# A two-layer retention and linear-attention backbone on one core: broadcast conditioning loads, three shift chunks on TensorE, another order of the first loads

## The chip, the cores and the metric

The kernel runs on one core of a Trainium2 chip, in one launch. The metric is the device time of the whole program in microseconds (us), the median of several runs. Five engines work beside each other, each on its own queue in order: TensorE (PE in the views; its weight loads are PEld), VectorE (DVE), ScalarE (ACT), GpSimd (POOL) and SyncE (SP). Here SP issues all data DMAs. PE writes into PSUM, and ACT and DVE empty it.

## What is computed

There are 256 context tokens and 512 latent tokens of width 1024, and two layers. Each layer starts with a modulated RMSNorm whose shift and scale (and later a gate) come from a conditioning vector, one for the context and one for the latents:

```python
def modulation(cvec, w_ada, b_ada):
    m = jax.nn.silu(cvec) @ w_ada + b_ada
    return jnp.split(m, 3, axis=-1)
...
        shift_x, scale_x, gate_x = modulation(c, w_ada[l], b_ada[l])
        shift_c, scale_c, gate_c = modulation(c_ctx, w_ada[l], b_ada[l])
        u_ctx = rms_norm(h_ctx, norm_gain[l]) * (1.0 + scale_c) + shift_c
        ctx_parts, ctx_states = token_mixers(u_ctx, w_in[l], ret_decay[l], gla_w_up[l], gla_b_up[l],
                                             None, zero_states)
```

One projection of the result feeds a retention branch and a gated linear attention branch, both bidirectional; they are normalised, gated, projected, merged, projected once more and added to the residual. A last RMSNorm gives the output. All of it is float32.

## The kernel before

**Layout.** Activations lie transposed: features on the 128 partitions, in 8 chunks of 128 (four pairs kp), tokens along the free dimension in three groups g of 256 (0 is the context) or six tiles of 128. A product in full precision is made of three products of split operands: `split` (L359) makes a high part on ACT (a copy, tiles `whi`, `streamh`) and the rest on DVE (`wlo`, `streaml`), and `mm3` (L315) issues high by high, low by high, high by low. Where no split pays, PE multiplies float32 operands directly (`mm`, L309).

**Order of the work.** Nothing runs as written. Generators hand operations to a planner, `Emit` (L221); it keeps a clock for each engine from its own cost estimates, takes the generators by priority and writes the operations out in the order in which they become ready by those clocks. On the chip each engine then runs its list in that order and waits only on semaphores. SP's list is in order too, and a load waits there for the eighth load before it (one semaphore lane each).

**The start, which the change touches.** `main` (L1597) issues `small` (biases and gains, and c as columns) and `cst` (the identity among others), then the twelve loads of x, 256 KB each (L1618 on), chunk pair by chunk pair and all three groups of each. `Norm.add` (L643) squares each piece on ACT and adds it up on DVE; `Norm.finish` (L662) sums over partitions on PE, takes the power on POOL and broadcasts it on PE. The modulation of layer 0 comes in four steps kp. For each, `ada_load` (L750) fetches eight pieces: two chunks of the transposed w_ada (`adat`, for the shift) and two chunks of w_ada (`adas`, for the scale). `ada_first` (L758) makes the scale on PE, as eight float32 products with the two silu(c) columns as weights (`op`), a copy of the two rows to SBUF on ACT and a turn of each chunk by the identity; the shift is made on DVE, as eight products with a sum (`ada_dve`, L742), for which silu(c) must stand in every partition. That is `load_c` (L724): 16 float32 products of 128 columns broadcast silu(c) over the partitions, ACT empties them, and four DMAs write them to DRAM, from which `ada_late` (L797) loads them again, three times in the program, for the other modulation chunks (all on DVE). `make_u` (L690) then scales x, applies mulc and mods on ACT and splits into `streamh`/`streaml`.

**The first projection.** `rproj_outer` (L1092) is the first user: for each chunk k of 8, and each of the six token tiles, one `mm3` of 512 columns, 144 matmuls in all, with three `pj` and three `xp` buffers of PSUM open at once. `ret_evac` (L1047) empties them. `Weights` (L502) loads weights by pieces of 512 KB into two buffers `wraw` and splits them into nine `whi`/`wlo` pairs. `decays` (L1001) and the tables R.tab (`ret_setup`, L1020) need ACT functions of other tables, so ACT_TABLE_LOADs. From there on the program is a long row of such projections, with the scans in between.

The places that say what a sentence can't:

```python
                for k in range(4):
                    e.mm(o[0][:, k], sc[:, 4 * half + k, v:v + 1].to_broadcast([P, P]), ident, True, True)
                t = cr[2 * v + half]
                e.copy(t[0], o[0].rearrange("p k n -> p (k n)"))
...
            yield dict(ev=ada_ev[1])
            decays()
            yield dict(ev=ada_ev[3])
```

Of the kernel before, what the change touches and what calls it, by code (L numbers as in the profile page):

```python
# [19 lines left out]
P = 128  # L20
D = 1024
KC = D // P
# [78 lines left out]


SMALL = {}
_o = 0
for _n, _w in (("bada", DEPTH * 24), ("ngain", DEPTH * KC), ("rgain", DEPTH * KC), ("ggain", DEPTH * KC), ("fgain", KC),
               ("decay", DEPTH * 2 * H), ("cT", KC * 2), ("kpos", DEPTH * 2 * H), ("zm", 3), ("wm", 2)):
    SMALL[_n] = (_o, _w)
    _o += _w
NSMALL = _o


def host_arrays(x, c, ctx, c_ctx, norm_gain, w_ada, b_ada, w_in, ret_decay, gla_w_up, gla_b_up, ret_norm_gain,
# [6 lines left out]
    a["adat"] = np.ascontiguousarray(w_ada.transpose(0, 2, 1)).reshape(DEPTH, 24, P, D)  # L119
    a["adas"] = np.ascontiguousarray(  # L120
        w_ada[0][:, D:2 * D].reshape(KC // 2, 2, P, 4, 256).transpose(3, 0, 2, 1, 4).reshape(4 * KC // 2, P, 512))
    small = np.zeros((P, NSMALL), f)

    def put(name, v):
        o, w = SMALL[name]
        small[:, o:o + w] = v
# [375 lines left out]
class Weights:  # L502


    def __init__(self, e, plan, src, begun):
        self.e, self.plan, self.src, self.begun = e, plan, src, begun
        e.spawn(self.run(), WEIGHTS)

    def run(self):
# [62 lines left out]
def body(ctx, tc, io, out):  # L572
# [148 lines left out]

    crd = []
# [35 lines left out]
    def ada_first(kp, C, A, ev, begun):  # L758

        yield dict(ev=[A.ev])  # L760

        def pe():
            yield dict(op=2, g=1, ev=begun)
            m = e.get("op", (256,))
            for k in range(KC):
                r = A.sraw[k // 2]
                e.mm(m[0][0:2], sc[:, k], r[0][:, k % 2], k == 0, k == KC - 1)
                if k % 2:
                    e.free(r)
            row = e.get("g", (256,))  # L770
            e.copy(row[0][0:2], m[0][0:2])
            e.free(m)
            o = e.get("op", (2, 2))
            for i in range(2):
                e.mm(o[0][:, i], row[0][0:2, i * P:i * P + P], ident[0:2, 0:2], True, True)
            e.free(row)
            a = 8 + 2 * kp
            e.tt(mods[0][:, a:a + 2], o[0], bada(0, a, 2), ADD)
            e.free(o)
            mod_scale(0, 2 * kp, 2 * kp + 2)  # L780
            e.done(ev[0])

        e.after(pe(), WEIGHTS)
        yield dict(g=1, ev=[C.ev])
        acc = v4(8).rearrange("p (i v f) -> p i v f", i=2, v=2)
        junk = e.get("g", (512,))
        for i in range(2):
            ada_dve(C.c, junk, A.traw[i], acc[:, i])
        e.free(junk)
        mv = mods[0][:, 2 * kp:2 * kp + 2]  # L790
        e.tt(mv, acc[:, :, :, 0], acc[:, :, :, 1], ADD)
        e.tt(mv, mv, bada(0, 2 * kp, 2), ADD)
        if kp == 3:
            e.free(*C.c)
        e.done(ev[1])
# [801 lines left out]
    def main():  # L1597
# [3 lines left out]
        for A in ada:  # L1601
            A.ev = Event()
        yield {}
# [5 lines left out]
        C = Obj()  # L1609
        C.ev = Event()  # L1610

        def cload():
            C.c = yield from load_c()
            e.done(C.ev)

        e.after(cload(), EVAC)
        hx = []
        for kp in range(4):  # L1618
            yield {}
            hx.append({})  # L1620
            for g in range(GROUPS):
                hx[kp][g] = e.get("g", (2, 256))
                e.dma(hx[kp][g][0], io["xT"][:, 2 * kp:2 * kp + 2, g * 256:g * 256 + 256])
                e.after(norm.add(g, kp, hx[kp][g][0]))
        u_ev = [{g: Event() for g in range(GROUPS)} for _ in range(4)]
        begun = [Event() for _ in range(4)]
        e.after(ada_load(0, ada[0], []))
        yield dict(ev=[ada[0].ev])
        w_ev = Event()
        Weights(e, plan, lambda key: io["w"][key[0], PIECE[key[1:]]], w_ev)  # L1630
        for kp in range(4):
            if kp:
                e.after(ada_load(kp, ada[kp], [w_ev]))
            e.after(ada_first(kp, C, ada[kp], ada_ev[kp], [begun[kp - 2]] if kp >= 2 else []))
            for g in range(GROUPS):
                e.after(make_u(0, kp, g, hx[kp][g], norm, u_ev[kp][g], ada_ev[kp], ada_ev[kp - 1] if kp else []))
# [98 lines left out]
```

## Time and profile before

| | |
|---|---|
| median of 3 runs | 1577.68 us (1577.55 to 1578.9) |
| the profiled execution, its own time | 1579.92 us |
| span of the profile | 1578.1 us |
| PE busy | 1551.5 us, 98% of the span |
| DVE, ACT, POOL busy | 1103.3, 823.6, 37.7 us |
| mean granted clock of TensorE | 0.994 |

The profile is of one execution. Its span runs from the first to the last instruction; its own time holds 1.8 us more around it. Times in the views are us from the start of the span. A line number in a view is mostly that of a helper (L312 is every matmul, L331 every ACT operation, L344 every tensor-tensor operation of DVE, L354 every fused one, L372 the power on POOL), so the tiles tell the operations apart. A float32 matmul stands in the trace as two instructions, and one of 128x512 with split operands as one. Matmuls overlap, so the pace is the distance of their starts.

### The profile page before, as it was taken

To read this page: it belongs to the slowest core of one execution; us is meant where nothing else is said; L and a number is where in the kernel's file an instruction comes from. 1 tells how busy PE (TensorE), PEld (TensorE's weight loads), DVE (VectorE), ACT (ScalarE), POOL (GpSimd) and SP (SyncE) were. 2 spreads that over 40 slices of the span, in tenths; PEclk is the share of its full clock that TensorE was granted. 3 is DMA by queue.
4 is the path that set the end of the run, shared out by engine and by line. 5 is a ranking of instruction groups with operands and counts; after the bars stand their busy time and mean duration, and the time that the engine had idled before them with its cause. 6 is when DMAs were issued, how large, how long until landed. Compare 5 with 4: busy or idle time off the path is not lost.

```text
span 1578.1 us, 24830 instructions
## 1 busy us (share of the span) xinstructions
PE 1551.5 (98%) x9284; PEld 1376.9 (87%) x9284; DVE 1103.3 (70%) x2628; ACT 823.6 (52%) x1778; POOL 37.7 (2%) x52
## 2 busy tenths in 40 slices
PE   7999999999999999999999999999999999999997
PEld 4788898988899999989888989988889899898887
DVE  7876495716878788776396765766657798878475
ACT  6734153521168787676333663443522868867453
POOL 0000000000000000000000000000000000000000
PEclk8999999999999999999999999999999999999999
DMA  9312021216731112112356421221355311223452
GB/s 353 131 47 68 34 81 54 94 60 205 228 109 54 61 48 67 38 58 94 129 205 209 139 81 60 94 81 41 121 187 174 121 49 60 81 64 97 167 184 90
DMA packets 73768, 170.32 MB, mean 108 GB/s; under 512 B 7728, under 2 KB 20144, under 8 KB 73648
## 3 DMA queue, kind: packets, MB, share of 16 engines
q1 hardware_dynamic: 73648, 168.74, 32.0%
q8 instruction: 73, 1.20, 0.3%
q14 instruction: 47, 0.39, 0.1%
HBM read 152.98 MB, written 15.73 MB: 107 GB/s over the span
## 4 chain that ended last, share of the span: by engine, by line
PE 91%; ACT 3%; issue 2%; DVE 2%; DMA 1%; POOL 0%; SPq 0%; POOLq 0%; DVEq 0%; ACTq 0%
PE pj L312 75%; PE xp L312 7%; PE op L312 6%; PE xp L321 2%; ACT g L331 1%; ACT whi L331 1%; DMA wraw<-in_w 1%; DVE g L344 1%; DMA g<-in_wup 0%; DVE p L344 0%; POOL v L372 0%; DVE wlo L344 0%; ACT p L331 0%; DMA g<-in_xT 0%; ACT L331 0%
## 5 line engine op out<-in xcount | busy, mean ns | idle before, releaser
L312 PE MATMUL pj<-streaml,whi 128*128 128x512 f32 (+1 forms) x1248 | 430.9, 345 | 0.6 <-DVE streaml L344 0.6
L312 PE MATMUL pj<-streamh,whi 128*128 128x512 f32 (+1 forms) x1248 | 430.5, 345 | 0.6 <-ACT g L331 0.6
L312 PE MATMUL pj<-streamh,wlo 128*128 128x512 f32 (+1 forms) x1248 | 430.7, 345 | 0.0
L331 ACT ACTIVATE whi<-wraw 128x512 fp32r<-128x512 f32 (+1 forms) x354 | 215.5, 619 | 246.1 <-PE pj L312 233.8
L344 DVE TENSOR_TENSOR wlo<-wraw,whi 128x512 fp32r<-128x512 f32 (+1 forms) x354 | 234.8, 675 | 154.7 <-ACT whi L331 153.9
L312 PEld LDWEIGHTS pj<-streamh,whi 128*128 128x128 f32 x1248 | 236.6, 190 | 25.5 <-ACT g L331 1.0
L312 PEld LDWEIGHTS pj<-streaml,whi 128*128 128x128 f32 x1248 | 236.7, 190 | 24.6 <-DVE streaml L344 0.8
L312 PEld LDWEIGHTS pj<-streamh,wlo 128*128 128x128 f32 x1248 | 236.5, 190 | 24.1
L312 PE MATMUL pj<-whi,streamh 128*128 128x256 f32 (+3 forms) x744 | 247.6, 333 | 0.6 <-ACT whi L331 0.6
L312 PE MATMUL pj<-wlo,streamh 128*128 128x256 f32 (+3 forms) x744 | 247.2, 332 | 0.3 <-DVE wlo L344 0.3
L312 PE MATMUL pj<-whi,streaml 128*128 128x256 f32 (+3 forms) x744 | 247.2, 332 | 0.0
L331 ACT ACTIVATE g<-g 128x512 f32<-128x512 f32 (+4 forms) x384 | 215.0, 585 | 59.0 <-DVE g L354 29.8
L331 ACT ACTIVATE g<-pj 128x256 f32<-128x256 f32 (+4 forms) x310 | 108.7, 387 | 245.5 <-PE pj L312 244.5
L344 DVE TENSOR_TENSOR g<-g,g 128x512 fp32r<-128x512 f32 (+5 forms) x368 | 193.4, 546 | 28.2 <-ACT g L331 24.8
L312 PE MATMUL pj<-g,whi 128*128 128x512 f32 (+1 forms) x768 | 204.0, 354 | 0.0
L312 PEld LDWEIGHTS pj<-g,whi 128*128 128x128 f32 x768 | 136.0, 189 | 20.3
L312 PEld LDWEIGHTS pj<-whi,streamh 128*128 128x128 f32 x744 | 140.9, 189 | 12.4 <-ACT whi L331 0.7
L312 PEld LDWEIGHTS pj<-wlo,streamh 128*128 128x128 f32 x744 | 140.8, 189 | 12.0 <-DVE wlo L344 0.5
L312 PEld LDWEIGHTS pj<-whi,streaml 128*128 128x128 f32 x744 | 140.8, 189 | 11.4 <-DVE streaml L344 0.3
L312 PE MATMUL xp<-g,g 128*128 128x256 f32 (+2 forms) x848 | 139.6, 278 | 0.1
L344 DVE TENSOR_TENSOR g<-pj,g 128x128 f32<-128x128 f32 (+3 forms) x165 | 59.6, 398 | 114.2 <-ACT g L331 113.8
L312 PE MATMUL pj<-g,wlo 128*128 128x512 f32 (+1 forms) x384 | 135.8, 354 | 0.0
(98 smaller groups left out, 1768.5 us busy)
## 6 DMA issues: line engine op xcount, KB each, us to landing
wraw<-in_w SPq DMA_DIRECT2D x177, 512.0 KB, 3.5
g<-in_adat SPq DMA_DIRECT2D x80, 256.0 KB, 5.1
g<-in_w SPq DMA_DIRECT2D x38, 256.0 KB, 5.8
g<-in_xT SPq DMA_DIRECT2D x24, 256.0 KB, 4.8
z<-g SPq DMA_DIRECT2D x20, 256.0 KB, 2.0
m<-g SPq DMA_DIRECT2D x20, 256.0 KB, 3.4
g<-m SPq DMA_DIRECT2D x20, 256.0 KB, 5.5
g<-in_adas SPq DMA_DIRECT2D x16, 256.0 KB, 5.6
```

Source lines behind the costliest of these rows:

```text
L312: self.op("pe", c, (l, r), (o,), lambda: self.nc.tensor.matmul(o, l, r, start=start, stop=stop))
L321: self.op("pe", 0.11, (i,), (o,), lambda: self.nc.tensor.transpose(o, i, ident))
L331: lambda: self.nc.scalar.activation(out=out, in_=in_, func=func, scale=scale, **kw), TABLE.get(func))
L344: lambda: self.nc.vector.tensor_tensor(out=out, in0=a, in1=b, op=op))
```

## The change

c comes from DRAM as a table `crow` of four rows of 512, and `load_c` reads each row into all 128 partitions with one DMA (a step of 0 over partitions); ACT then applies silu to the four tiles. The products, copies and writes to DRAM are gone; `ada_late` does the same load and silu each time. `PE_SHIFT = (0, 1, 2)`: shift chunks 0, 1 and 2 of layer 0 are made on PE beside the scale chunks of their step, so the PE product of step 0 has 512 columns, that of step 1 has 384, and those of steps 2 and 3 stay at 256. The tables `adas0` to `adas3` hold these columns. The first loads come in another order: x of the context group, step 0's PE columns, one weight piece, x of the two latent groups, `crow`, then steps 1 to 3; the second weight piece comes after step 1's loads. `decays` waits for step 3.

```diff
+PE_SHIFT = (0, 1, 2)
...
+def pe_chunks(kp):
+
+    return [oc for oc in (2 * kp, 2 * kp + 1) if oc in PE_SHIFT] + [8 + 2 * kp, 9 + 2 * kp]
...
+    a["crow"] = np.stack([c_ctx, c[0]], 0).reshape(4, 512)
...
         yield {}
-        for _ in range(SLOTS["wraw"]):
+        load()
+        e.done(self.begun)
+        yield dict(ev=[self.second])
+        for _ in range(SLOTS["wraw"] - 1):
             load()
-        e.done(self.begun)
...
-    def load_c():
-
-        yield dict(g=4)
-        cr = [e.get("g", (512,)) for _ in range(4)]
-        for v in range(2):
-            for half in range(2):
-                yield dict(pj=1)
-                o = e.get("pj", (4, P))
-                for k in range(4):
-                    e.mm(o[0][:, k], sc[:, 4 * half + k, v:v + 1].to_broadcast([P, P]), ident, True, True)
-                t = cr[2 * v + half]
-                e.copy(t[0], o[0].rearrange("p k n -> p (k n)"))
-                e.free(o)
-                d = e.dram("c")
-                e.dma(d, t[0])
-                crd.append(d)
-        return cr
+    def load_c(cr):
+
+        for i, t in enumerate(cr):
+            src = io["crow"]
+            e.dma(t[0], bass.AP(tensor=src.tensor, offset=src.offset + 512 * i, ap=[[0, P], [1, 512]]))
+        for t in cr:
+            e.act(t[0], t[0], AF.Silu)
...
     def ada_load(kp, A, wait):
-        yield dict(g=8, ev=wait)
-        A.traw = [halves(io["adat"][0, 2 * kp + i]) for i in range(2)]
-        A.sraw = [e.get("g", (2, 256)) for _ in range(KC // 2)]
-        for i in range(KC // 2):
-            e.dma(A.sraw[i][0].rearrange("p k n -> p (k n)"), io["adas"][4 * kp + i])
+
+        n = len(pe_chunks(kp)) * P
+        per = 512 // n
+        yield dict(g=KC // per + 2 * (4 - n // P), ev=wait)
+        for oc in (2 * kp, 2 * kp + 1):
+            if oc not in PE_SHIFT:
+                A.rows[oc] = halves(io["adat"][0, oc])
+        A.cols = [e.get("g", (per, n)) for _ in range(KC // per)]
+        for i, r in enumerate(A.cols):
+            e.dma(r[0].rearrange("p k n -> p (k n)"), io[f"adas{kp}"][:, i * per * n:(i + 1) * per * n])
         e.done(A.ev)
...
+    def ada_pe(kp, cols, ev, begun):
+
+        ocs = pe_chunks(kp)
+        n = len(ocs) * P
+        per = 512 // n
+        yield dict(op=2, g=1, ev=begun)
+        m = e.get("op", (n,))
+        for k in range(KC):
+            r = cols[k // per]
+            e.mm(m[0][0:2], sc[:, k], r[0][:, k % per], k == 0, k == KC - 1)
+            if k % per == per - 1:
+                e.free(r)
+        row = e.get("g", (n,))
+        e.copy(row[0][0:2], m[0][0:2])
+        e.free(m)
+        o = e.get("op", (len(ocs), 2))
+        for i in range(len(ocs)):
+            e.mm(o[0][:, i], row[0][0:2, i * P:i * P + P], ident[0:2, 0:2], True, True)
...
     def ada_late(todo, done, then=None):
 
         yield dict(g=5)
-        cr = []
-        for d in crd:
-            t = e.get("g", (512,))
-            e.dma(t[0], d)
-            cr.append(t)
+        cr = [e.get("g", (512,)) for _ in range(4)]
+        load_c(cr)
...
         if l == 0:
-            yield dict(ev=ada_ev[1])
+            yield dict(ev=ada_ev[3])
             decays()
-            yield dict(ev=ada_ev[3])
+            yield {}
...
+        yield from load_x(0)
         e.after(ada_load(0, ada[0], []))
+        e.after(ada_first(0, C, ada[0], ada_ev[0], []))
         yield dict(ev=[ada[0].ev])
-        w_ev = Event()
-        Weights(e, plan, lambda key: io["w"][key[0], PIECE[key[1:]]], w_ev)
+        Weights(e, plan, lambda key: io["w"][key[0], PIECE[key[1:]]], w_ev, ada[1].ev)
+        yield dict(ev=[w_ev])
+        yield from load_x(1)
+        yield from load_x(2)
+        e.done(x_ev)
+        yield dict(ev=[C.ev])
```

Where the instructions stand now, as the two programs list them (the number after a tile's name is a running number; x of the context is `g_91`, `g_93`, ...).

SP, the first loads, of each run of like loads the first; before (12 x, 4 adat, 4 adas, 2 weight pieces, 4 adat, 4 adas follow each other):

```order
L375 DMA g_91<-in_xT 128x2x256
L375 DMA g_136<-in_adat 128x512
L375 DMA g_140<-in_adas 128x512
L375 DMA wraw_152<-in_w 128x1024
L375 DMA g_158<-in_adat 128x512
L375 DMA g_162<-in_adas 128x512
```

and now (4 x, 8 adas, 1 weight piece, 8 x, 4 crow, 2 adat, 8 adas, 1 weight piece, then steps 2 and 3):

```order
L383 DMA g_91<-in_xT 128x2x256
L383 DMA g_104<-in_adas 128x512
L383 DMA wraw_123<-in_w 128x1024
L383 DMA g_126<-in_xT 128x2x256
L383 DMA g_151<-in_crow 128x512
L383 DMA g_242<-in_adat 128x512
L383 DMA g_244<-in_adas 128x384
L383 DMA wraw_262<-in_w 128x1024
L383 DMA g_275<-in_adat 128x512
```

The PE columns of step 0 moved ahead of eight loads of x and of all of adat; the four loads of `crow` now stand between the loads of step 0 and those of step 1.

PE, up to the first matmul of the first projection (`pj_331`); before:

```order
L312 MATMUL xp_310<-cst,v_87_277 128x128 x2
L312 MATMUL op_167<-g_140,sc 2x256 x2
L312 MATMUL op_169<-cst,g_168 128x2 x2
L312 MATMUL op_363<-g_162,sc 2x256 x2
L312 MATMUL op_363<-g_165,sc 2x256 x2
L312 MATMUL pj_387<-whi_156,streamh_78 128x512
```

and now (of the eight products of each step the first two and the last, 2x512 for step 0 and 2x384 for step 1):

```order
L320 MATMUL op_120<-g_104,sc 2x512
L320 MATMUL xp_171<-ones,p_96 128x2 x2
L320 MATMUL op_120<-g_105,sc 2x512
L320 MATMUL xp_179<-cst,v_46_173 128x128 x2
L320 MATMUL op_120<-g_111,sc 2x512
L320 MATMUL op_122<-cst,g_121 128x2 x4
L320 MATMUL op_270<-g_244,sc 2x384
L320 MATMUL xp_327<-cst,v_56_235 128x128 x2
L320 MATMUL op_270<-g_245,sc 2x384
L320 MATMUL op_270<-g_251,sc 2x384
L320 MATMUL pj_331<-whi_264,streamh_78 128x512
```

In both lists the products of steps 0 and 1 stand ahead of the first projection; step 0's now stand ahead of most of the norm's small products, and the last norm broadcast (`xp_327`) stands between the first and the second product of step 1.

ACT, where it begins to empty the first projection; before, the tables R.tab (`g_649` to `g_651`) stood ahead and in between:

```order
L331 ACTIVATE g_651<-g_652,lg 128x128
L331 ACTIVATE whi_729<-wraw_618 128x512
L331 ACTIVATE g_649<-p_726 128x128
L331 ACTIVATE g_650<-g_652,lg 128x128
L331 ACTIVATE g_738<-pj_387 128x256
```

and now they stand behind, with two table loads:

```order
L339 ACTIVATE whi_685<-wraw_563 128x512
L339 ACTIVATE g_691<-pj_331 128x256
L339 ACTIVATE g_730<-xp_432 128x256
L339 ACT_TABLE_LOAD
L339 ACTIVATE g_781<-pj_741 128x256
L339 ACT_TABLE_LOAD
L339 ACTIVATE g_670<-p_674 128x128
```

Over the whole program PE issues 8 float32 products of 256 columns each for steps 2 and 3 as before, 8 of 512 and 8 of 384 where there were 16 of 256, three more turns, and 16 products of 128 fewer; DVE 12 fused products of 128x512 fewer; ACT 16 silu of 128x512 more, 4 copies fewer and 59 table loads where there were 53; SP 4 writes and 12 loads of c fewer, 16 loads of `crow` more, 6 of adat (256 KB) fewer and 8 of adas (192 KB) more.

## Rows read from the trace of the kernel before

**Rows 1.** The page's part 1: busy time, share of the span, instructions.

```profile
PE 1551.5 (98%) x9284; PEld 1376.9 (87%) x9284; DVE 1103.3 (70%) x2628; ACT 823.6 (52%) x1778; POOL 37.7 (2%) x52
```

**Rows 2.** Waits of PE, 80 to 1500 us: in total, times, longest.

```profile
PE xp L321 <- ACT g L331: 3.3, 7, 1.2
```

**Rows 3.** The chain that ended last, in order of time: start, us, what.

```profile
2.64 4.60 DMA g<-in_xT
17.38 1.08 POOL v L372
18.51 1.24 PE xp L312 x4
31.10 1.05 PE pj L312 x3
33.58 0.69 PE pj L312 x3
34.27 3.55 PE op L312 x16
```

**Rows 4.** PE in order of time: start, us, instruction [idle before <-releaser].

```profile
4.39 5.20 PE L312 MATMUL pj<-cst,sc 128*128 128x128 f32 x32 [4.39 <-DMA cst<-in_cst]
14.30 2.72 PE L312 MATMUL xp<-ones,p 128*128 128x2 f32 x12 [4.71 <-DVE p L344]
21.42 5.03 PE L312 MATMUL op<-g,sc 128*2 128x256 f32 x16
26.96 0.60 PE L312 MATMUL op<-cst,g 2*128 2x2 f32 x4 [0.51 <-ACT g L331]
31.03 0.50 PE L312 MATMUL pj<-whi,streamh 128*128 128x512 f32 x1
73.54 0.39 PE L312 MATMUL xp<-whi,streaml 128*128 128x512 f32 x1
74.51 0.36 PE L312 MATMUL pj<-streamh,whi 128*128 128x256 f32 x1 [0.58 <-ACT g L331]
```

**Rows 5.** ACT in order of time, the same columns.

```profile
13.33 0.63 ACT L331 ACTIVATE g<-g 128x512 f32<-128x512 f32 x1 [0.22 <-DMA g<-in_xT]
13.87 0.58 ACT L331 ACTIVATE g<-pj 128x512 f32<-128x512 f32 x1
21.80 1.66 ACT L331 ACTIVATE whi<-wraw 128x512 fp32r<-128x512 f32 x3
27.99 2.08 ACT L331 ACTIVATE g<-g,mod,mulc 128x256 f32<-128x256 f32 x4 [1.09 <-DVE mulc L354]
43.20 1.15 ACT L331 ACTIVATE whi<-wraw 128x512 fp32r<-128x512 f32 x2 [0.40 <-DMA wraw<-in_w]
```

**Rows 6.** DVE in order of time, the same columns.

```profile
8.92 6.96 DVE L344 TENSOR_TENSOR p<-p,g 128x256 f32<-128x256 f32 x18 [0.58 <-ACT g L331]
22.00 1.29 DVE L344 TENSOR_TENSOR wlo<-wraw,whi 128x512 fp32r<-128x512 f32 x2
35.30 0.69 DVE L354 SCALAR_TENSOR_TENSOR g<-g,g 128x512 f32<-128x512 f32 x1
```

**Rows 7.** Stretches: length, busy us (instructions) of PE, PEld, DVE, ACT, POOL, PEclk, DMA share, GB/s.

```profile
6.00:7.00 1.00, 1.00 (x7) 1.00 (x6) 0.18 (x2) 0.63 (x1) 0.00 (x0) 1.00 1.05 353
8.00:9.00 1.00, 1.00 (x11) 1.00 (x11) 0.42 (x2) 1.00 (x3) 0.00 (x0) 1.00 0.95 327
17.00:18.00 1.00, 0.02 (x1) 0.00 (x0) 0.98 (x6) 0.00 (x0) 0.62 (x1) 0.50 1.07 393
23.00:24.00 1.00, 1.00 (x4) 0.32 (x3) 1.00 (x4) 0.46 (x1) 0.00 (x0) 0.50 1.06 391
25.00:26.00 1.00, 1.00 (x6) 0.41 (x5) 1.00 (x4) 0.00 (x0) 0.00 (x0) 1.00 1.03 381
73.67:1500.00 1426.33, 1420.97 (x8523) 1268.56 (x8522) 995.99 (x2366) 738.23 (x1612) 33.62 (x43) 1.00 0.30 99
```

**Rows 8.** ACT's groups by shape, 80 to 1578 us: count, busy, mean ns.

```profile
L331 ACT ACT_TABLE_LOAD x48 | 61.6, 1283 | 0.8
```

More of the change, by code (lines that the diff above doesn't have):

```diff
@@ L119, in host_arrays @@
     a["adat"] = np.ascontiguousarray(w_ada.transpose(0, 2, 1)).reshape(DEPTH, 24, P, D)
-    a["adas"] = np.ascontiguousarray(
-        w_ada[0][:, D:2 * D].reshape(KC // 2, 2, P, 4, 256).transpose(3, 0, 2, 1, 4).reshape(4 * KC // 2, P, 512))
+    for kp in range(4):
+        w = np.concatenate([w_ada[0][:, oc * P:oc * P + P] for oc in pe_chunks(kp)], 1)
+        a[f"adas{kp}"] = np.ascontiguousarray(w.reshape(KC, P, -1).transpose(1, 0, 2).reshape(P, -1))
     small = np.zeros((P, NSMALL), f)
@@ L502, with __init__ @@
 class Weights:
-    def __init__(self, e, plan, src, begun):
-        self.e, self.plan, self.src, self.begun = e, plan, src, begun
+    def __init__(self, e, plan, src, begun, second):
+        self.e, self.plan, self.src, self.begun, self.second = e, plan, src, begun, second
         e.spawn(self.run(), WEIGHTS)
@@ L720, in halves @@
         return r
-    crd = []
-    def load_c():
-        yield dict(g=4)
-        cr = [e.get("g", (512,)) for _ in range(4)]
-        for v in range(2):
-            for half in range(2):
-                yield dict(pj=1)
-                o = e.get("pj", (4, P))
-                for k in range(4):
-                    e.mm(o[0][:, k], sc[:, 4 * half + k, v:v + 1].to_broadcast([P, P]), ident, True, True)
-                t = cr[2 * v + half]
-                e.copy(t[0], o[0].rearrange("p k n -> p (k n)"))
-                e.free(o)
-                d = e.dram("c")
-                e.dma(d, t[0])
-                crd.append(d)
-        return cr
+    def load_c(cr):
[4 more added lines that the diff above has]
+            e.act(t[0], t[0], AF.Silu)
     def ada_dve(cr, junk, raw, acc):
@@ L750, in ada_load @@
     def ada_load(kp, A, wait):
-        yield dict(g=8, ev=wait)
-        A.traw = [halves(io["adat"][0, 2 * kp + i]) for i in range(2)]
-        A.sraw = [e.get("g", (2, 256)) for _ in range(KC // 2)]
-        for i in range(KC // 2):
-            e.dma(A.sraw[i][0].rearrange("p k n -> p (k n)"), io["adas"][4 * kp + i])
-        e.done(A.ev)
-    def ada_first(kp, C, A, ev, begun):
-        yield dict(ev=[A.ev])
[L762 to L792, printed above, removed]
@@ new lines, in ada_load @@
+        n = len(pe_chunks(kp)) * P
[7 more added lines that the diff above has]
+            e.dma(r[0].rearrange("p k n -> p (k n)"), io[f"adas{kp}"][:, i * per * n:(i + 1) * per * n])
+        e.done(A.ev)
+    def ada_pe(kp, cols, ev, begun):
[15 more added lines that the diff above has]
+            e.mm(o[0][:, i], row[0][0:2, i * P:i * P + P], ident[0:2, 0:2], True, True)
+        e.free(row)
+        ns = len(ocs) - 2
+        e.tt(mods[0][:, ocs[ns]:ocs[ns] + 2], o[0][:, ns:], bada(0, ocs[ns], 2), ADD)
+        mod_scale(0, 2 * kp, 2 * kp + 2)
+        if ns:
+            e.tt(mods[0][:, ocs[0]:ocs[0] + ns], o[0][:, :ns], bada(0, ocs[0], ns), ADD)
+        e.free(o)
+        e.done(ev)
@@ new lines, in ada_first @@
+    def ada_first(kp, C, A, evs, begun):
+        yield dict(ev=[A.ev])
+        e.after(ada_pe(kp, A.cols, evs[0], begun), WEIGHTS)
+        if A.rows:
+            yield dict(g=1, ev=[C.ev])
+            junk = e.get("g", (512,))
+            for oc in sorted(A.rows):
+                acc = v4(4).rearrange("p (v f) -> p v f", v=2)
+                ada_dve(C.c, junk, A.rows[oc], acc)
+                mv = mods[0][:, oc]
+                e.tt(mv, acc[:, :, 0], acc[:, :, 1], ADD)
+                e.tt(mv, mv, sm("bada", oc, 1).to_broadcast([P, 2]), ADD)
+            e.free(junk)
+            e.done(evs[1])
+        else:
+            e.done(evs[1])
@@ L793, in ada_first @@
         if kp == 3:
             e.free(*C.c)
-        e.done(ev[1])
     def ada_late(todo, done, then=None):
         yield dict(g=5)
-        cr = []
-        for d in crd:
-            t = e.get("g", (512,))
-            e.dma(t[0], d)
-            cr.append(t)
+        cr = [e.get("g", (512,)) for _ in range(4)]
+        load_c(cr)
         junk = e.get("g", (512,))
@@ L1601, in main @@
         for A in ada:
-            A.ev = Event()
+            A.ev, A.rows = Event(), {}
         yield {}
@@ L1609, in main, with load_x @@
         C = Obj()
-        C.ev = Event()
+        C.ev, w_ev, x_ev = Event(), Event(), Event()
         def cload():
-            C.c = yield from load_c()
+            yield dict(g=4, ev=[x_ev])
+            C.c = [e.get("g", (512,)) for _ in range(4)]
+            load_c(C.c)
             e.done(C.ev)
[L1616 to L1621, printed above, removed]
+        e.after(cload())
+        hx = [{} for _ in range(4)]
+        def load_x(g):
+            for kp in range(4):
+                yield {}
                 hx[kp][g] = e.get("g", (2, 256))
@@ L1626, in main @@
         begun = [Event() for _ in range(4)]
+        yield from load_x(0)
         e.after(ada_load(0, ada[0], []))
+        e.after(ada_first(0, C, ada[0], ada_ev[0], []))
         yield dict(ev=[ada[0].ev])
-        w_ev = Event()
-        Weights(e, plan, lambda key: io["w"][key[0], PIECE[key[1:]]], w_ev)
+        Weights(e, plan, lambda key: io["w"][key[0], PIECE[key[1:]]], w_ev, ada[1].ev)
[4 more added lines that the diff above has]
+        yield dict(ev=[C.ev])
         for kp in range(4):
             if kp:
-                e.after(ada_load(kp, ada[kp], [w_ev]))
-            e.after(ada_first(kp, C, ada[kp], ada_ev[kp], [begun[kp - 2]] if kp >= 2 else []))
+                e.after(ada_load(kp, ada[kp], []))
+                e.after(ada_first(kp, C, ada[kp], ada_ev[kp], [begun[kp - 2]] if kp >= 2 else []))
             for g in range(GROUPS):
```

## The prediction

> **What bounds the kernel now.** The page's part 1 comes first: PE is busy 98% of the span [rows 1]. The waits of PE show that between 80 and 1500 us its largest loss is 3.3 us, to ACT, in seven waits [rows 2]. So a change at the start can only gain or lose what it does to the moment at which PE begins its unbroken row of work, and to the few gaps behind it. The timeline of PE gives that moment: the first matmul of the first projection starts at 31.03, and the last of its 144 starts at 73.54 [rows 4]. In between PE never waits, but it also does the modulation products of steps 2 and 3 there, before and after the change alike. Behind it stands one gap, 0.58 us ahead of 74.51, put down to ACT [rows 4].
>
> Before 31.03 the loads set the pace: the DMA engines' share is about one in every stretch shown of the first 26 us [rows 7]. Then comes PE's clock. Its rate was low up to some point near 7 us (7 records a us, 11 later [rows 7]), although the column says 1.00 there; it is 0.50 at 17 and 23 us and 1.00 at 25 us. 1.00 and 0.50 are the levels of 2.4 and 1.2 GHz. PE became busy at 4.39 and at 18.51 [rows 3, 4], so it became fast about 3 and about 6 us after that; it fell after it had idled from 9.6 on.
>
> **Where the loads land now.** The third x load lands at 2.64 + 4.60 = 7.24 [rows 3] and the eleventh at 13.33, where its square waited for it [rows 5]: 6.09 / 8 = 0.76 us each. From there to the weight piece that ends a wait at 43.20 [rows 5] SP's list holds 47 pieces of 256 KB: 0.64 us each. The changed list then lands as follows. x of the context by 8.0; step 0's eight pieces from 8.6 to 13.1; the weight piece at 14.4; the other x at 20.5; `crow` from 21.1 to 23.0; two of adat at 24.3; step 1's eight, three quarters as large, from 24.8 to 28.2. Before, step 1's last piece was the 32nd of 256 KB in SP's list, now it is the 34th, 1.3 us later; PE came to it late then, from the norm's work and step 0, and now it is the last thing that the first projection waits for.
>
> For `crow` no row shows a load that reads one DRAM row into all partitions. Below, I bound it by a gain of the whole 2.6 us; above, by 4.60 us each, the way of one load from issue to landing [rows 3], 18.4 us for the four. I take 0.64, since what is written per load is what every other load writes, and the engines that write it were already full [rows 7].
>
> The Trainium skill (DMA: Bandwidth & Descriptors, "Latency and other measured facts") states that loads whose partition rows lie far apart at large powers of two fell from 214 to 103 GB/s, and offers one HBM channel serving them all as an unverified reason. No run here shows such a pitch; all partitions reading one row would be a near relative, and a factor of two would make the sum about 1.6 us larger. It is the first rival below, priced there from rows.
>
> **Step 0 on PE.** Eight float32 products of 256 columns took 3.55 us at full clock [rows 3], 0.444 each; 512 columns cost 0.89 and 384 cost 0.67, twice that at 1.2 GHz. The first starts at 8.6, slow: 10.4. The norm's first small product follows (4 of 12 records in 2.72 us [rows 4]): 11.3. The second product, slow: 13.1. The norm broadcast, whose power took 1.08 on POOL [rows 3]: 14.3 with the 1.24 us of rows 3. Six more at full clock, since PE has been busy for 6 us: 19.6 (25.0 if slow). The row copy costs 0.58 [rows 5], four turns at 0.30 [rows 4] 1.2: 21.4. So scale and shift of step 0 are there early and wait for ACT.
>
> **ACT and DVE to the first operand.** ACT squares the last latent x (landed at 20.5; 0.55 each, as the copies at 21.80 are spaced [rows 5]): 22.6. Three silu: 24.2; the norm's copy and the fourth silu: 25.2. Then two scalings of 0.52 [rows 5], two weight splits and the activation split: 27.9. DVE's part of that split (0.65 [rows 6]) ends at about 29. This is no longer than the loads.
>
> **Step 1 on PE, which sets the end.** Its first product starts at 24.8, slow: 26.1. Next in the list is the last norm broadcast. Its sum stands on DVE behind the adds of that group (0.39 each [rows 6]) and behind a fused product (0.70 [rows 6]) that waits for silu: 26.3; POOL: 27.4; the broadcast about 1.0: 28.4. All seven remaining products have landed by then. At full clock they end at 33.1, at 1.2 GHz at 37.7. By the 3 and 6 us above, the clock comes back between 27.8 and 30.8, so none or two of the seven are slow: 33.1 to 34.4. I take the middle, 33.8. The first projection starts at 33.8 in place of 31.03.
>
> **The sum.** Later start: +2.8. The first three matmuls took 1.05 us where three take 0.69 [rows 3], a wait for the operand that the later start covers: -0.36. Step 1 turns three chunks in place of two: +0.3. The gap of 0.58 us at 74.51: ACT had twelve table operations of R.tab around the first evacuations, and now has them behind, so it should go: -0.58. Together **+2.1 us**.
>
> The other edits cost nothing. The 16 products for c (5.20 us of PE [rows 4]) ended before PE had other work, and the four writes of c only took DMA time (4 x 0.64 = 2.6 us) that the four loads of `crow` take again. DVE's twelve fused products fewer (12 x 0.70 = 8.4 us) and the later `decays` relieve engines on which PE waits nowhere between 32 and 73 us, so they give nothing; if the first projection did wait for its operands there, up to these 8.4 us would be the relief. ACT gets 12 silu and 6 table loads (1.28 each [rows 8]) inside the PE-bound part: 2.2 + 1.3 to 2.6 us at each of three places. They lie beside a block of 24 matmuls at 0.23 us, 5.5 us, and ACT idles 688 of 1426 us there [rows 7]. If that cover is gone, they cost up to 4.8 us at a place.
>
> Against the profiled execution's own time this makes 1579.92 + 2.1 = 1582.0. That execution stood 2.2 us above the median of the runs shown; against the median it is 1577.68 + 2.1 = **1579.8 us**. A measurement here tells about 0.2%, 3.2 us, from no change.
>
> **The rivals.**
>
> *The broadcast load is slow* (ends slower). All 128 partitions read the same 2 KB. For it: no row shows such a load at full rate. Against it: the bytes written are the usual ones. Every us that the four take beyond 2.6 moves the rest of the list; the first us only fills PE's pause for the norm broadcast, every further one is lost. At twice the price +3.7 us; at four times (7.7 more) +8.8, 1586.5, and the late ones, on which silu and so ACT would wait in its order, come on top. It decides above some 1.8 times the price. Chance 0.17 for beyond that point.
>
> *PE's clock stays at 1.2 GHz through step 1.* For it: PE idles between 21 and 24.8 but for norm products, and pauses at 26. Against it: twice before PE became fast within 6 us. The start becomes 37.7 and the sum +6.0, 1583.7. Chance 0.07.
>
> *The late silu hold ACT up.* ACT works in order, so a late `crow` load or two switches of table delay the weight splits behind. Against it: only 3.3 us lost to ACT in 1420 us [rows 2]. One place uncovered: +4.8, sum +6.9, 1584.6. Chance 0.06.
>
> *PE keeps up with the loads* (ends faster). Were the clock high and the norm broadcast early, the projection would start with the last landing, 28.2 + 0.67, or with its operand at 29: -2.0 - 0.36 + 0.3 - 0.58 = -2.6, 1575.1. For more than 0.2% the loads would have to land half a us earlier too. Chance 0.07 for that; it is also the case in which the change does what its order of loads suggests, a projection that starts earlier.
>
> **How the numbers follow.** My forecast, a shift of at most 0.2% either way with +2.1 as its middle, has 0.63. The three slower rivals have 0.17 + 0.07 + 0.06 = 0.30, the faster one 0.07. The range goes from 1576.5 (a start at 30.5) to 1584.5, which takes in the all-slow clock and a broadcast load of up to twice the price; beyond it lie the four-fold price above and the full gain below, together under 0.2.
>
> **What would show it.** Right: the first `pj` matmul between 33 and 34.5; step 1's products of 384 columns with their last one ending there, the first ones at twice the duration of the last; `crow` loads landing 0.64 apart, the silu after them near 23; no ACT gap at the end of the first projection; the same waits of PE after 80 us. Wrong: `crow` loads several us apart; a start before 31; a wait of PE on ACT behind the late silu; a projection that pauses once it has begun.

## The result, and the profile after

The changed kernel takes 1599.41 us (median of 4 runs, 1599.12 to 1600.15); the kernel before took 1577.62 us beside it (4 runs). The ratio is 1.0136, with a 95% interval of 1.0124 to 1.0148: slower by 21.8 us, where 2.1 us were forecast. The profiled execution's own time is 1599.59 us and its span 1597.8 us. The mean granted clock is 0.994, as before.

Part 1 of the page answers to [rows 1]. PE is busy 98% of the span again, with 26 instructions fewer, yet for 20 us more:

```profile
PE 1571.8 (98%) x9258; PEld 1372.4 (86%) x9258; DVE 1096.7 (69%) x2608; ACT 840.2 (53%) x1796; POOL 38.1 (2%) x52
```

So the time did not go into waits. The waits of PE between 80 and 1500 us confirm it; the largest is smaller than in [rows 2] (columns: total us, times, longest us):

```profile
PE xp L329 <- ACT g L339: 2.1, 6, 0.5
PE pj L320 <- DVE wlo L352: 0.4, 1, 0.4
```

**The start.** PE's timeline (start us, us, engine line op out<-in; in brackets idle before and its releaser) answers to [rows 3, 4]:

```profile
9.06 1.86 PE L320 MATMUL op<-g,sc 128*2 128x512 f32 x2 [9.06 <-DMA g<-in_adas]
...
14.75 6.63 PE L320 MATMUL op<-g,sc 128*2 128x512 f32 x12
22.05 1.05 PE L320 MATMUL op<-cst,g 2*128 2x2 f32 x8 [0.68 <-ACT g L339]
23.03 0.61 PE L320 MATMUL xp<-ones,p 128*128 128x2 f32 x4
25.25 1.22 PE L320 MATMUL xp<-cst,v 128*128 128x128 f32 x4 [1.62 <-POOL v L380]
26.27 0.96 PE L320 MATMUL xp<-ones,p 128*128 128x2 f32 x4
27.16 1.44 PE L320 MATMUL op<-g,sc 128*2 128x384 f32 x2
29.79 1.23 PE L320 MATMUL xp<-cst,v 128*128 128x128 f32 x4 [1.19 <-POOL v L380]
30.94 6.42 PE L320 MATMUL op<-g,sc 128*2 128x384 f32 x14
37.30 0.50 PE L320 MATMUL pj<-whi,streamh 128*128 128x512 f32 x1
```

The first projection starts at 37.30, not at 31.03. PE pauses from 23.6 to 25.25 and from 28.6 to 29.8. The windows show its granted clock (the column after POOL): it falls in the first pause and comes back only near 34.5:

```profile
21.00:24.00 3.00, 1.96 (x13) 1.48 (x12) 1.29 (x6) 2.59 (x6) 0.00 (x0) 1.00 1.04 385
24.00:25.00 1.00, 0.00 (x0) 0.00 (x0) 0.93 (x4) 1.00 (x3) 0.73 (x1) 0.63 1.07 379
25.00:30.00 5.00, 3.56 (x11) 2.16 (x12) 4.86 (x13) 4.12 (x10) 1.26 (x2) 0.50 1.06 383
30.00:35.00 5.00, 5.00 (x12) 1.58 (x13) 5.00 (x11) 3.48 (x7) 0.00 (x0) 0.55 1.05 387
35.00:37.00 2.00, 2.00 (x8) 0.46 (x6) 2.00 (x7) 0.00 (x0) 0.00 (x0) 1.00 1.06 384
```

**The rest.** From the first projection to the end the kernel before took 1578.1 - 31.03 = 1547.1 us; now it is 1597.8 - 37.30 = 1560.5. That is 13.4 us more, in the part that the change hardly touches. The chain in order of time shows where: nearly everywhere. Here are three pieces of the chain in which PE works without a break (start us, us, what, number of instructions), first of before, then of after:

```profile
172.96 28.13 PE pj L312 x124
741.06 144.32 PE pj L312 x774
1521.83 23.77 PE pj L312 x196
```

```profile
179.94 28.83 PE pj L320 x124
750.47 146.76 PE pj L320 x774
1542.27 23.53 PE pj L320 x196
```

The first piece holds 512-column matmuls (all but one): 28.13 / 124 = 227 ns each before, 28.83 / 124 = 232 ns after, at the same granted clock of 1.00 and with no wait. The last piece holds 256-column ones, which became a little faster (121 to 120 ns). The program has 3840 of the 512-column matmuls with split operands, before and after alike. A slower pace of every one of them is a thing for which the prediction had no term.

A small part of the 13.4 us is of another kind. In this execution the granted clock was 0.50 from 925.4 to 928.8 us, and the piece of the chain there is 1.4 us longer than in a_psum, a run below with the same instructions and the same pace, whose clock stayed at 1.00 there (of after, then of a_psum):

```profile
925.77 27.25 PE pj L320 x117
925.75 25.83 PE pj L320 x117
```

### The profile page after: what moved, and what is told of

It is laid out like the page before. It is cut to its first block, busy times and chain, and to the rows that moved or that the text cites. A ratio compares the mean times of both kernels' runs of the same rounds, so it can differ in the third digit from the quotient of the medians.

```text
span 1597.8 us, 24772 instructions
## 1 busy us (share of the span) xinstructions
PE 1571.8 (98%) x9258; PEld 1372.4 (86%) x9258; DVE 1096.7 (69%) x2608; ACT 840.2 (53%) x1796; POOL 38.1 (2%) x52
## 4 chain that ended last, share of the span: by engine, by line
PE 94%; issue 2%; DMA 2%; DVE 1%; ACT 1%; POOL 1%; SPq 0%; POOLq 0%; DVEq 0%
PE pj L320 78%; PE xp L320 8%; PE op L320 6%; PE xp L329 2%; DMA g<-in_xT 1%; POOL v L380 1%; DMA g<-in_adas 1%; DVE g L352 0%; DMA g<-in_adat 0%; ACT p L339 0%; ACT g L339 0%; DVE wlo L352 0%; ACT whi L339 0%; DVE streaml L352 0%; DVE v L357 0%
## 5 line engine op out<-in xcount | busy, mean ns | idle before, releaser
L339 ACT ACTIVATE g<-g 128x512 f32<-128x512 f32 (+4 forms) x400 | 224.4, 586 | 60.1 <-DVE g L362 29.6
L339 ACT ACTIVATE g<-pj 128x256 f32<-128x256 f32 (+3 forms) x306 | 106.4, 385 | 249.2 <-PE pj L320 248.4
L320 PEld LDWEIGHTS pj<-wlo,streamh 128*128 128x128 f32 x744 | 140.8, 189 | 13.4 <-DVE wlo L352 0.7
```

Of the source, the lines that this page charges most:

```text
L320: self.op("pe", c, (l, r), (o,), lambda: self.nc.tensor.matmul(o, l, r, start=start, stop=stop))
L339: lambda: self.nc.scalar.activation(out=out, in_=in_, func=func, scale=scale, **kw), TABLE.get(func))
```

## The experiments

### Where whi and wlo stand

The compiled programs differ in more than their instructions. The allocator places tiles in the order in which the program first asks for them. In the kernel before, the small `v4` tiles (14 of 64 bytes) came after `whi` and `wlo`. With the context's x loaded first, the norm of the context asks for `v4` ahead of the first weight split, so `whi` and `wlo` moved up by 14 x 64 = 896 bytes. And since the products of c no longer use `pj` first, the PSUM banks were dealt out anew, and `pj` lost its banks 0 to 2. Theory A blames the first, theory B the second, theory C the order or number of instructions. Each of the three kernels here differs from its parent in addresses alone. Run a_sb:

```diff
+    for tag, n in (("g", 51), ("p", 8), ("wraw", 2), ("whi", 9), ("wlo", 9)):
+        for _ in range(n):
+            (ps if tag in PSUM else sb).tile([P, WIDTH.get(tag, 16)], F32, name=e.name(tag), tag=tag, bufs=n)
     e.spawn(main(), MAIN)
```

> The changed kernel with the tiles whi and wlo at their SBUF addresses of before (896 bytes lower; the small v4 tiles stand behind them again); every instruction and its order as in the changed kernel. Theory A, the split weights' place in SBUF sets the pace of the 512-column matmuls: their start-to-start goes from 232 back to 227 ns, 3779 of them win 4.5 ns each (17 us) and the 256-column ones lose 0.9 ns each (some 3 us), so 1599.4 - 14 = about 1585.5 us; what stays is the later start, about +6. Theory B, PSUM banks, and theory C, the order or number of instructions: no change, 1599.4 us within 2, median distance 232 ns.

Run a_psum has the same lines with `(("pj", 3), ("op", 2), ("xp", 3))`.

> The changed kernel with pj, op and xp in the PSUM banks that they had before (pj 0 to 2, op 3 and 4, xp 5 to 7); every instruction and its order as in the changed kernel, SBUF as in the changed kernel. Theory B (PSUM banks set the pace): about 1585.5 us and 227 ns for 512 columns. Theory A (SBUF place of whi and wlo) and theory C (order of instructions): 1599.4 us within 2, and 232 ns.

Run b_896 has them in the kernel before, with `(("g", 51), ("p", 8), ("wraw", 2), ("v4", 14))`.

> The kernel before with whi and wlo 896 bytes higher in SBUF (the v4 tiles in front of them), every instruction and its order as in the kernel before. Theory A: the pace of the changed kernel, 232 ns for 512 columns, and 1577.6 + 14 = about 1591.6 us. Theories B and C: 1577.6 us within 2, and 227 ns.

Measured: a_sb 1583.87 us, a_psum 1598.83, b_896 1592.08, beside 1577.93 of before. The same pieces of the chain, of a_sb, of a_psum and of b_896 in that order:

```profile
177.12 28.14 PE pj L320 x124
743.85 144.32 PE pj L320 x774
1524.82 23.78 PE pj L320 x196
```

```profile
180.05 28.82 PE pj L320 x124
750.57 146.77 PE pj L320 x774
```

```profile
173.59 28.82 PE pj L312 x124
744.09 146.76 PE pj L312 x774
1534.04 23.53 PE pj L312 x196
```

Theory A holds in both directions and B and C fall: the pace follows the addresses of `whi` and `wlo`, to 0.02 us in 28. The 896 bytes cost 1599.41 - 1583.87 = 15.5 us in the changed kernel and 1592.08 - 1577.93 = 14.2 us in the kernel before. The 15.5 us hold some chance of the start: in the profiled executions it lies at 35.81 in a_sb and at 37.30 in the changed kernel. From the first projection to the end a_sb takes 1545.7 us, 13.8 less than the 1559.5 of a_psum.

### Which distance is good

Run b_map32 takes the kernel before and sets its nine `whi` and nine `wlo` tiles at nine offsets.

```diff
-SLOTS = {"g": 51,
+SLOTS = {"g": 50,
-"whi": 512, "wlo": 512,
+"whi": 520, "wlo": 520, "pad": 56,
+    for tag, n in (("g", 50), ("p", 8), ("wraw", 2), ("whi", 9), ("pad", 1), ("wlo", 9)):
+        for _ in range(n):
...
```

> The kernel before with 50 instead of 51 tiles g, and the nine whi and nine wlo tiles each 32 bytes further apart, so that they stand at 0, 32, 64, ... 256 bytes (whi and wlo alike) from the place modulo 512 that they had. One look at the pace of the 512-column matmuls by the tile they read. Theory A: the distance depends on the tile, 227 ns at 0 and at 256 bytes, 232 ns at 128 bytes, and it shows which other offsets are as good or better. Theories B and C: the same 227 ns for all nine. The time itself is of no interest, since one g tile fewer may cost some us; between 1575 and 1600 us.

It took 1596.3 us (one run). The table is worked out from the starts in its trace: the distance to the next start, over pairs of 512-column matmuls after 90 us of which the first has tile i of `whi` or `wlo` as its weights (some 260 to 300 pairs each). The trace leaves out the buffers' numbers; which tile a matmul reads follows from the order in which the program takes the tiles. In the kernel before, the tiles shown by the same count have 228 to 229 ns, with a median of 227.

| offset, bytes | 0 | 32 | 64 | 96 | 128 | 160 | 192 | 224 | 256 |
|---|---|---|---|---|---|---|---|---|---|
| mean, ns | 229.2 | 233.3 | 231.6 | 234.3 | 230.8 | 233.3 | 230.5 | 233.0 | 228.4 |
| median, ns | 227 | 233 | 231 | 234 | 230 | 232 | 231 | 233 | 227 |

Only 0 and 256 have the pace of before; 128 came out at 231, a little better than expected and better than the 232 of the changed kernel, whose shift of 896 bytes lies 128 beyond a multiple of 256; why is open. No other offset beats 0 and 256. Where the tile is the moving operand the map is less clear (232.4 ns at 0, 229.3 at 256), perhaps because each such tile is in use for a few matmuls only, between tiles of other offsets. Two runs with one number changed each then put the rule to the test: a_v4_16 in the changed kernel and b_abs96 in the kernel before.

```diff
-        return e.ring("v4", n, 16, 14)
+        return e.ring("v4", n, 16, 16)
```

> The changed kernel with 16 instead of 14 of the small v4 tiles, that is 1024 in place of 896 bytes in front of whi and wlo, every instruction and its order as in the changed kernel. By what the map showed (good places are 256 bytes apart), whi and wlo stand 1024 bytes from their place of before and the pace of before comes back: 227 ns for 512 columns, and 1584 us as in the run a_sb. If only the very addresses of before were good, or the distance modulo 2048: 232 ns and 1599 us.

```diff
+    e.const([P, 24], F32, "pad")
     small = e.const([P, NSMALL], F32, "small")
```

> The kernel before with every tile from the constants on 96 bytes higher in SBUF, so that all large tiles start at a multiple of 128 bytes where they started at an odd multiple of 32, and their distances from each other stay; every instruction and its order as in the kernel before. If only the distance between the tiles that one matmul reads matters: 227 ns and 1577.9 us within 2. If the place by itself matters: another pace, either way, 5 us or more.

Measured: 1583.27 us for a_v4_16 (ratio to before 1.0035, 1.0021 to 1.0048) and 1578.14 for b_abs96 (1.0000, 0.9991 to 1.0009). The long piece of the chain in each:

```profile
744.85 144.32 PE pj L320 x774
```

```profile
739.42 144.32 PE pj L312 x774
```

So it is the distance between the tiles that counts, not the place: a shift of all tiles by 96 bytes changes nothing, and `whi` and `wlo` may move by 1024 bytes but not by 896. That 256 bytes are enough rests on the map alone, since no run moves `whi` and `wlo` by 256 or 512 bytes. The sizes of all large tiles of the kernel before are multiples of 1024 bytes, and so are the distances between them; it had the good placement without a line that asks for it. Two `v4` tiles more give the changed kernel 16 of its 22 us back.

### What made the start late

What is left is the start: 35.81 in a_sb. Two parts of the change could be at fault, the wide products on PE (S) and the order of the loads (L). All four runs have the addresses of a_sb. Run a_noshift:

```diff
-PE_SHIFT = (0, 1, 2)
+PE_SHIFT = ()
```

> The changed kernel with whi and wlo at their SBUF addresses of before (as in the run a_sb, 1583.9 us, whose first projection starts at 35.8), and with no shift chunk on TensorE: all products of the four steps have 256 columns, and DVE makes all eight shift chunks. What is left of the slowdown is the later start. Theory S (the wider products of steps 0 and 1 on TensorE make the start late): step 1's products win 8 x 0.22 us at full clock and up to twice that at half, the start comes 2 to 3 us earlier, 1581 to 1582 us. Theory L (the order of loads makes it late): the start stays within 1 us of 35.8, or comes later because DVE has 12 more fused products of 0.7 us ahead of its splits; 1583.5 to 1588 us.

Run a_noorder (a_crow is both edits together):

```diff
-        def load_x(g):
-            for kp in range(4):
+        def load_x(kp):
+            for g in range(GROUPS):
...
-        yield from load_x(0)
+        for kp in range(4):
+            yield from load_x(kp)
+        e.done(x_ev)
+        yield dict(ev=[C.ev])
         e.after(ada_load(0, ada[0], []))
         e.after(ada_first(0, C, ada[0], ada_ev[0], []))
         yield dict(ev=[ada[0].ev])
-        Weights(e, plan, lambda key: io["w"][key[0], PIECE[key[1:]]], w_ev, ada[1].ev)
+        Weights(e, plan, lambda key: io["w"][key[0], PIECE[key[1:]]], w_ev, ada[0].ev)
         yield dict(ev=[w_ev])
-        yield from load_x(1)
-        yield from load_x(2)
-        e.done(x_ev)
-        yield dict(ev=[C.ev])
```

> As the run a_sb, but the first loads stand in the order of before: all twelve x loads pair by pair, the four loads of crow, step 0, two weight pieces, steps 1 to 3; the three shift chunks stay on TensorE. Theory L: the start comes back to 31.5 to 33, and the time to about 1580 to 1581 us. Theory S: the start stays at 35 to 37, about 1583.9 us.

> As the run a_sb, with both undone: order of loads of before, no shift chunk on TensorE. What is left of the change is the broadcast load in place of the 16 products and the copies of c, at the start and three times later. If the broadcast load is worth nothing, good or bad, 1577.9 us within 2 and a start between 30 and 32.5. If the four loads at the head of the queue or the late silu cost something, 2 to 5 us more.

Run a_warm:

```diff
         e.free(o)
         e.done(ev)
+        if kp == 0:
+            yield dict(op=1)
+            o = e.get("op", (256,))
+            for k in range(5):
+                e.mm(o[0][0:2], sc[:, k], cst[:, 0:2].rearrange("p a b -> p (a b)"), k == 0, k == 4)
+            e.free(o)
```

> As the run a_sb, with five float32 products of 256 columns more behind step 0's turns (their result is used by nothing), so that TensorE has full work between 23 and 26 us, where its clock fell. Theory of the clock (half of it is what makes step 1 late): the granted clock stays at 1.00 or comes back before 31 us, step 1's last seven products take 4.7 us in place of 6.0, and the start comes 1 to 2.5 us earlier, 1581.5 to 1583 us, though the five products hold up the norm's broadcast by up to 1.5 us. If the clock does not matter: the start comes 0 to 1.5 us later, 1584 to 1585.5 us.

| run | us | ratio to before, 95% | first projection starts |
|---|---|---|---|
| a_sb | 1583.87 | 1.0035 (1.0022 to 1.0048) | 35.81 |
| a_noshift | 1589.69 | 1.0078 (1.0065 to 1.0090) | 40.63 |
| a_noorder | 1581.49 | 1.0019 (1.0011 to 1.0028) | 34.42 |
| a_crow | 1579.36 | 1.0010 (1.0002 to 1.0019) | 33.66 |
| a_warm | 1581.72 | 1.0023 (1.0014 to 1.0032) | 34.40 |

Theory S falls, and a_noshift went past what either theory allowed. Its timeline shows a long wait:

```profile
40.63 0.79 PE L320 MATMUL pj<-whi,streamh 128*128 128x512 f32 x1 [5.35 <-ACT streamh L339]
```

With `crow` late in the list, DVE's shift for step 0 comes late too, and PE waits for the operand that ACT makes from it. During the wait the clock fell a second time, to 0.50 from 38.9 to 49.1 us, and the stretch behind the start took 1548.7 us. In the new order of loads the shift chunks on PE are thus needed; in the old order (a_noorder against a_crow) they cost 1581.49 - 1579.36 = 2.1 us. Theory L is half right: the old order wins 2.4 us, but the start came back to 34.4 and not to 33. The clock has no part in that: in a_noorder the granted clock is 1.00 from 21 us through the whole first projection. Its products of steps 0 and 1, wider by the shift chunks, take 7.26 and 5.32 us, where those of before took 5.03 and 3.62. The start of a_crow, 33.66, also lies outside the 30 to 32.5 expected, its time within.

In the new order the clock is the other half. In a_warm PE's timeline and clock read:

```profile
23.24 3.24 PE L320 MATMUL op<-cst,sc 128*2 128x256 f32 x8
...
29.15 0.71 PE L320 MATMUL xp<-cst,v 128*128 128x128 f32 x4 [0.24 <-POOL v L380]
29.79 4.68 PE L320 MATMUL op<-g,sc 128*2 128x384 f32 x14
34.40 0.50 PE L320 MATMUL pj<-whi,streamh 128*128 128x512 f32 x1
```

```profile
23.00:24.00 1.00, 1.00 (x6) 0.52 (x6) 0.96 (x6) 1.00 (x3) 0.06 (x1) 0.81 1.04 382
24.00:27.00 3.00, 3.00 (x9) 1.11 (x8) 2.83 (x7) 2.42 (x5) 0.87 (x1) 0.50 1.07 375
27.00:28.00 1.00, 1.00 (x9) 0.82 (x9) 0.81 (x4) 0.57 (x3) 0.00 (x0) 0.98 1.08 377
```

The clock still falls, but with work under way from 21.7 on it is back at 27, where in a_sb it came back near 32.5 and in the changed kernel near 34.5. Seven products in 4.68 us are 0.67 each, full clock. Five useless products won some 2 us (1583.87 to 1581.72, each beside its own runs of before; the two intervals in the table overlap). In a_crow, step 1 waits 2.04 us for its loads (behind those of `crow`), and the clock is 0.50 again from 30 to 33.

The broadcast loads themselves were ordinary. The sixteen of them in the changed kernel:

```profile
L383 SPq DMA_DIRECT2D g<-in_crow x16: 328/422/433, 15.6 to 1179.5; - x16
...
  ACT g L339: 5.2, 4
...
DMA to landing us min/median/max: 4.4/5.6/7.6
```

They land in a median of 5.6 us (the four at the start 5.8), the x loads in 6.1, and the windows above show 379 to 387 GB/s throughout. The four at the start landed 0.7 us apart, from 21.6 to 23.6. ACT waited 5.2 us in all for the late ones, and the waits of PE shown above have no trace of it.

### A version faster than both

Run b_warm keeps PE at work in the kernel before; `fill(n)` makes n float32 products of 256 columns into an `op` tile.

```diff
             e.rsqrt(r, ms, expo)
+            if self.warm:
+                yield from fill(2)
...
         e.after(cload(), EVAC)
+        e.after(fill(8), EVAC)
+        norm.warm = True
```

> The kernel before with TensorE kept at work between the products of c and step 1: eight float32 products of 256 columns behind the products of c and two behind each group's sum (their results are used by nothing; the planner then puts step 0's products ahead of the norm's broadcasts). It is a try for a version faster than both. If the clock is what can still be won at the start: the granted clock is 1.00 from 8 to 31 us, step 0's products take 3.6 us in place of 5.0, the first projection starts at 29 to 30 in place of 31.0, and the time is 1576 to 1577 us. If the loads or DVE and ACT stand right behind the clock: start 30.5 to 32, 1577.5 to 1579 us.

1580.54 us (1.0016, 1.0007 to 1.0025): slower. The clock fell at 19 us all the same, step 0's products took 5.30 us, and the planner put the norm's broadcasts behind them, so that PE waited for ACT at 32.44. This run tells that useless work in the wrong place costs more than the clock gives; it does not tell what a clock of 1.00 would have given.

Run b_late takes the other way. From the first projection to the end, the runs with the change and the good placement take 1544.5 to 1545.7 us (a_noshift with its second fall of the clock apart), the kernel before 1547.1 and, moved by 96 bytes, 1576.1 - 30.27 = 1545.8.

```diff
-                d = e.dram("c")
-                e.dma(d, t[0])
-                crd.append(d)
...
-        for d in crd:
-            t = e.get("g", (512,))
-            e.dma(t[0], d)
-            cr.append(t)
+        cr = [e.get("g", (512,)) for _ in range(4)]
+        for i, t in enumerate(cr):
+            src = io["crow"]
+            e.dma(t[0], bass.AP(tensor=src.tensor, offset=src.offset + 512 * i, ap=[[0, P], [1, 512]]))
+        for t in cr:
+            e.act(t[0], t[0], AF.Silu)
...
-            yield dict(ev=ada_ev[1])
+            yield dict(ev=ada_ev[3])
             decays()
-            yield dict(ev=ada_ev[3])
+            yield {}
```

> A try for a version faster than both, of the kernel before (its order of loads, all shift chunks on DVE, silu(c) spread by TensorE at the start, SBUF and PSUM places of before), with the two parts of the change that touch nothing ahead of the first projection: the later users of c load crow by broadcast and apply silu (the four writes of c to DRAM are gone), and decays waits for step 3. In the runs with the change and the good placement the stretch from the first projection to the end took 1544.5 us, in the kernel before 1546 to 1547. If that gain comes from these two parts: start 30.3 to 31.5, 1575.5 to 1577 us. If it belongs to the shift chunks on TensorE or to the order of loads: 1577.5 to 1578.5 us.

1576.93 us, beside 1578.49 of before in the same session: 0.9990 (0.9981 to 0.9999). Its start:

```profile
25.65 3.71 PE L313 MATMUL op<-g,sc 128*2 128x256 f32 x16
30.27 0.50 PE L313 MATMUL pj<-whi,streamh 128*128 128x512 f32 x1 [0.91 <-ACT streamh L332]
```

The stretch behind it is 1575.0 - 30.27 = 1544.7 us, that of the changed runs. So two parts of the change are together worth some 1.6 us, with an interval that just leaves out zero; in the stretch it is 1.1 to 2.4 us, as the two executions with the instructions of before differ. No run parts the two.

## Why the prediction was wrong, point by point

**The step that failed first** is the sum itself: "a change at the start can only gain or lose what it does to the moment at which PE begins its unbroken row of work, and to the few gaps behind it". The work behind the start was taken as fixed. The runs a_sb, a_psum and b_896 show a third thing that such a change can move, the addresses, and with them the pace of 3840 matmuls, 227 ns each before and 232 after: some 14 to 15.5 of the 21.8 us. No rival had it. The rows could not show it, since the kernel before holds one placement only. The two lists of addresses would have shown that something moved, though not what it costs.

**The start** was forecast at 33.8 and came at 37.30 (35.81 to 37.44 in four kernels with the same instructions). Here the path was right and two terms were too small. The first, 2.5 of the 3.5 us: step 1's last seven products began behind the last norm broadcast at 30.94, not at 28.4. Step 0 ended 1.6 us late (its turns near 23.0, forecast 21.4), mostly because its "six more at full clock" took 6.63 us and not 5.3: its products started 1.7 us apart at first and 0.86 apart only from 17.8 us on. The norm's other broadcast, the last sum and step 1's first product stood ahead of the last broadcast at half clock, and DVE's queue held POOL up until 28.66. The second, the remaining 1.0 us: "the clock comes back between 27.8 and 30.8" was wrong. It came back at 34.5; PE had paused again from 28.6 to 29.8. So some three of the seven products were slow, and they took 6.42 us where full clock gives 4.68 and the forecast had 5.4.

The rival of a clock at 1.2 GHz through step 1, a start of 37.7 and 1583.7 us at a chance of 0.07, is near what came about in its number: without the placement the changed kernel takes 1583.3 to 1583.9 us. That it is so near is in part luck, since all seven products were to be slow there and the late broadcast had no part in it. It deserved a larger chance, because the clock's two quick rises in the trace of before both followed work without a pause.

**Right were** the loads (first product at 9.06, forecast 8.6; the last x at 20.9, forecast 20.5, which takes 0.76 us for each of the eight x and not the 0.64 that the text takes for the rest), the price of `crow` (0.7 us each, forecast 0.64; rival one fell), the late silu (PE lost nothing to them, rival three fell), and the gap of [rows 4] at the end of the first projection: the 144 matmuls and what lies between take 42.8 to 42.9 us in a_sb and a_v4_16, against 43.48 with the gap before. The first operand was to be ready at about 29 and came near 31, hidden behind step 1. PE never caught up with the loads, so the faster rival fell too.

**Where rule and trace differ.** The Trainium skill (TensorE: Matmul & The Clock Gate, "Wait — 56ns, not 53.3ns?") gives 215.7 ns from start to start for 512 columns at the high clock. Here it is 227 ns in one placement and 232 in the other, so some 11 and 17 ns above that figure. The measurement decides, and the prediction rightly took its pace from rows.

## What to carry to other kernels

A change that adds, drops or reorders first uses of tiles also moves every tile allocated later: compare the addresses of the two programs, and where PE bounds the kernel, keep the distances between the large operands at multiples of a good step, for instance by rounding up the small pools in front of them (here 1024 bytes of shift were harmless, and by the map 256 are too). When busy time grows without waits, look at the distance between starts in an unbroken row, and test it with a kernel that changes addresses alone. Before a PE-bound stretch, pauses on TensorE can cost twice: here two of 1.6 and 1.2 us as idle time, and a clock of 0.50 until 34.5 us beside and behind them.

## What the runs showed of the hardware

- The pace of 512-column matmuls depends on the distance in SBUF between the tiles that they read: 227 ns at the distances of before and 1024 bytes further, 232 at 896 bytes further, at the same clock; in the map the medians are 227 ns at 0 and 256 bytes and 230 to 234 at the other multiples of 32. It holds whichever tile is the weight: grouped by shape, the mean of one 512-column matmul goes from 393 to 396 ns where the stream tiles stand first in the row's name, and from 392 to 397 where `whi` does. For 256 columns it goes slightly the other way (23.78 against 23.53 us for 196). Why the distance matters is open: weight loads do overlap matmuls in the trace (PEld is busy 86% of the span beside PE's 98%), but no run shows that the two get in each other's way.
- In the good placement the starts lie 227, 227, 226 ns apart, over and over; in the other they wander between 228 and 241 ns in a repeating pattern.
- The clock's return is not a fixed time after work resumes: it took some 6 us in the kernel before (18.51 to 24.3) and 9 us (25.25 to 34.5) in the changed one, whose PE paused in between; in a_warm, where PE kept working, it was back 3 us after it fell.
